# A hybrid RG-LRU / band-attention layer on one core: a fourth plain up pair, other memory and ScalarE order for deferred blocks, a tail without GpSimd

## The chip, the core and the metric

The kernel runs on one NeuronCore of a Trainium2 chip. The metric is the device time of one execution in microseconds; smaller is better. The times below are runs of the kernel before, and one further execution was recorded by the profiler.

## What is computed

One layer of a streaming encoder, for 1024 prompt tokens and 64 sample tokens, all in 32-bit floats:

- u = x·(1 + scale1(c)) + shift1(c), then z = u @ w_in, split into seven sections of 1024 columns.
- Branch A is a gated linear recurrence behind a short convolution, branch B is attention over a band of chunks; x1 = LN(α·x + (1 + gate1)·(merged @ w_out)).
- u2 = x1·(1 + scale2(c)) + shift2(c), then y = LN(α·x1 + (1 + gate2)·(relu(u2 @ w_up + b_up)² @ w_down + b_down)).

The change lies in the last line, the feed-forward part: w_up is 1024 x 4096 and w_down 4096 x 1024. Keys, values and recurrence states are outputs too; the change does not touch them.

## The kernel before

The 1088 tokens are cut into three groups of 384, 384 and 320 (g = 0, 1, 2); features lie on the 128 partitions, in blocks of 128. Every product is made of three matmuls on numbers split into a high and a low part (`mm3`, L109 to L112): high·high, high·low, low·high. A split is a ScalarE copy into the high part and a VectorE subtraction for the low part: for weights L97 and L98 in `wsplit`, for other data L103 and L104 in `split`. `wsplit` also issues the load of the weight block on SP (L93).

**The up product (L610 to L826).** The 32 blocks of w_up's columns are handled as 16 pairs p. Pairs 0 and 1 run beside the end of the first layer norm. Then `up_pair` (L782) takes p = 2 to 15. For groups 0 and 1 a pair is a 2 x 2 product of matrices (two weight blocks by two token groups), which is done in one of two ways:

- a *plain* pair (p < PLAIN, here only p = 2): four products c11, c12, c21, c22 over all 8 feature blocks, each 24 matmuls of 384 columns, each followed by bias, relu and square on ScalarE (`relu2`, L616 and L617);
- a *Strassen* pair: seven products of 12 matmuls (`strassen`, L759), on sums of weights (`wops`, L725: four GpSimd additions L741 to L745, and two more splits) and on sums of tokens, the T tiles of L692 to L720. The products go to banks x, z, x, y, x, y, x, and the product k = 2 adds to bank x after ScalarE has copied x away (L801, L806, L808).

The T tiles are made once, in two halves q, by VectorE additions (L704 to L719) and splits. `vsums` holds one instruction of each half; `tc.issue_after(ins)` means that what the block issues on the engine of `ins` is queued behind `ins` on it (order only, no wait for its end). So plain weights are queued on VectorE behind the first half's x = y - x (L712), Strassen weights behind the second half's.

Group 2 (320 tokens) of each pair goes through `up_g2` (L771): two products ug of 24 matmuls, relu and square into a tile cg, and a store of it into `hg_d` on the ScalarE queue. For groups 0 and 1 `put_pair` (L629) makes the GpSimd sums t1 to t4 and stores seven operands into `hs_d`, four from the GpSimd queue and three from the ScalarE queue.

**The down product (L829 to L911).** It adds up 32 blocks into accumulators: `fg` for group 2, `facc` for groups 0 and 1, loaded from `facc_d` and first scaled and shifted by ScalarE (L863, L900). Group 2's down blocks are the *deferred blocks* of this text: `down_g2` (L848) runs twice, for chunks c = 0, 1 ahead of the Strassen part and for c = 2, 3 behind it. A call goes over r = 0, 1 (four accumulators each), the two chunks and b = 0 to 3; each of its 16 blocks dg is 24 matmuls of 320 columns on one weight block wh_dg, wl_dg and on the operand halves ophg, oplg, which `load_hg` (L843) loads from `hg_d` on SP and splits. Pair 15 (LATE) is special: its `up_g2` is called at L878, after the first two `load_hg`, so TensorE has work while the down product starts.

**Order and memory.** The order on each engine is drawn up at build time by a scheduler, which places each instruction by its readiness in an estimate and by program order; engines run their queue in order. The tiles of the pool `hp` (L829) lie over memory that the up product's pools used: each new tile waits for the last readers of the bytes under it. `hp` gives out memory in the order in which tags are first asked for: facc, opr, oph, opl, then cg, which LATE's `up_g2` takes from `spool[0]`, and so on.

**The tail (L959 to L973).** Behind the last down blocks `final2` normalises group 2's three token tiles (c = 0, 128, 256): for columns 512 and up two VectorE operations (L967, L968) and a store on the ScalarE queue; for the lower half ScalarE's scaling (L966), a multiplication and an addition (L971, L972), by GpSimd for c = 0 and by VectorE else, and a store on SP (L973). The power in the layer norm's moments (L530) is GpSimd's.

Of the kernel before, what the change touches and what calls it, by code (L numbers as in the profile page):

```python
# [11 lines left out]
F32 = mybir.dt.float32  # L12
R32 = mybir.dt.float32r
AF = mybir.ActivationFunctionType
ALU = mybir.AluOpType
PSUM = bass.MemoryType.PSUM

P = 128
# [7 lines left out]
TW2 = 320  # L26
# [22 lines left out]
def body(nc, tc, a):  # L49
    V, S, G, TE, SY = nc.vector, nc.scalar, nc.gpsimd, nc.tensor, nc.sync  # L50
    with ExitStack() as es:
# [34 lines left out]
        for g in range(3):  # L86
            uh[g], ul[g] = newact(g, f"uh{g}"), newact(g, f"ul{g}")

        wlast = [None]

        def wsplit(src, nm, pool=None, tags=("whi", "wlo")):
            raw = wp.tile([P, NB, P], F32, tag="wraw", name=f"wr_{nm}")
            wlast[0] = SY.dma_start(raw, src).ins  # L93
            bufs = 2 if pool else 3
            hi = (pool or wp).tile([P, NB, P], R32, tag=tags[0], bufs=bufs, name=f"wh_{nm}")
            lo = (pool or wp).tile([P, NB, P], R32, tag=tags[1], bufs=bufs, name=f"wl_{nm}")
            S.activation(hi, raw, AF.Copy)  # L97
            V.tensor_tensor(lo, raw, hi.bitcast(F32), op=ALU.subtract)  # L98
            return hi, lo

        def split(hi, lo, src, scl=None):
            if scl is None:
                S.activation(hi, src, AF.Copy)  # L103
                V.tensor_tensor(lo, src, hi.bitcast(F32), op=ALU.subtract)  # L104
            else:
                S.activation(hi, src, AF.Copy, scale=scl)
                V.scalar_tensor_tensor(lo, src, scl, hi.bitcast(F32), op0=ALU.mult, op1=ALU.subtract)
# [591 lines left out]
        for q in range(2):  # L699
            k2 = slice(2 * q, 2 * q + 2)  # L700
            x, y, z = tts.pop() if tts else tt3(q)

            def join(d, b):
                V.tensor_tensor(d, whole(b[0][:, k2, :]), whole(b[1][:, k2, :]), op=ALU.add)  # L704

            def tsplit(k, src):
                split(ut[k][0][:, k2, :], ut[k][1][:, k2, :], src)

            join(x, b11)
            join(y, b12)  # L710
            join(z, b22)
            vsums.append(V.tensor_tensor(x, y, x, op=ALU.subtract).ins)  # L712
            V.tensor_tensor(y, z, y, op=ALU.subtract)
            V.tensor_tensor(z, z, x, op=ALU.subtract)
            tsplit(2, z)
            tsplit(1, x)
            join(x, b21)
            tsplit(3, y)
            V.tensor_tensor(x, x, z, op=ALU.subtract)  # L719
            tsplit(4, x)  # L720
        uops = [b11, b21, ut[2], ut[1], ut[3], b22, ut[4]]

# [48 lines left out]
        def up_g2(p, wa, wb):  # L771
            for b, (wt, f) in enumerate(zip((wa, wb), fblocks(p))):
                ps = acc(f"ug{p}_{b}")
                for kb in range(NB):
                    mm3(ps[:, :TW2], wt[0][:, kb, :], wt[1][:, kb, :], u2h[2][:, kb, :], u2l[2][:, kb, :], kb == 0, kb == NB - 1)
                c = spool[0].tile([P, TW2], F32, tag="cg", bufs=2, name=f"cg{p}_{b}")
                relu2(c, ps[:, :TW2], f)
                put_g2(p, b, c)

        PLAIN, LATE = 3, 15  # L780

        def up_pair(p):  # L782
            f1, f2 = fblocks(p)
            c11, c12, c21, c22 = (new_t(f"c{p}_{k}") for k in range(4))
            if p < PLAIN:
                with tc.issue_after(vsums[0]):
                    wa, wb = up_w(f1), up_w(f2)
                for c, f, g, (wh, wl) in ((c11, f1, 0, wa), (c12, f1, 1, wa), (c21, f2, 0, wb), (c22, f2, 1, wb)):
                    ps = acc(f"up{f}_{g}")
                    for kb in range(NB):  # L790
                        mm3(ps[:, :GW], wh[:, kb, :], wl[:, kb, :], u2h[g][:, kb, :], u2l[g][:, kb, :], kb == 0, kb == NB - 1)
                    relu2(c, ps[:, :GW], f)
                up_g2(p, wa, wb)
                put_pair(p, c11, c12, c21, c22, [], new_t)
                return
            with tc.issue_after(vsums[1]):
                w, wa, wb = wops(a["w_up"][f1], a["w_up"][f2], f"u{p}_", True)

            def after(k, ps):
                if k == 0:  # L800
                    S.activation(c11, ps, AF.Copy)  # L801
                elif k == 1:
                    V.tensor_tensor(c11, ps, c11, op=ALU.add)
                    relu2(c11, c11, f1)
                elif k == 2:
                    S.activation(c12, ps, AF.Copy)  # L806
                elif k == 3:
                    S.activation(c22, ps, AF.Copy)  # L808
                elif k == 4:
                    V.tensor_tensor(c22, ps, c22, op=ALU.add)  # L810
                    relu2(c22, c22, f2)
                elif k == 5:
                    V.tensor_tensor(c12, ps, c12, op=ALU.add)
                    relu2(c12, c12, f1)
                else:
                    relu2(c21, ps, f2)

            strassen(w, uops, f"u{p}", after)
            put_pair(p, c11, c12, c21, c22, [], new_t)
            if p == LATE:  # L820
                return wa, wb
            up_g2(p, wa, wb)
# [10 lines left out]
        def new_facc(fb):  # L833
            return hp.tile([P, TS2], F32, tag=f"facc{fb}", name=f"facc{fb}")

        facc = {fb: new_facc(fb) for fb in range(4)}

        def op_split(src, nm):
            hl = [hp.tile(list(src.shape), R32, tag=t, bufs=7, name=f"{t}{nm}") for t in ("oph", "opl")]
            split(*hl, src)  # L840
            return hl

        def load_hg(c, h):  # L843
# [4 lines left out]
        def down_g2(cs, hg, after):  # L848

            for r in range(2):  # L850
                ps = [acc(f"dg{4 * r + b}_{cs[0]}") for b in range(4)]
                for c in cs:
                    for b in range(4):
                        with tc.issue_after(loads[1]):
                            wh, wl = wsplit(a["w_down"][c, 4 * r + b], f"dg{r}_{c}_{b}")
                        if b == 1 and (c + 1, 0) not in hg and c + 1 in cs:
                            with tc.issue_after(wlast[0]):
                                hg.update({(c + 1, h): load_hg(c + 1, h) for h in range(2)})
                            with tc.issue_after(loads[-1]):
                                SY.dma_start(fg, facc_d[:, :, TS2:T])  # L860
                            for fb in range(NB):
                                for c0, c1, w in parts(2):
                                    S.activation(fg[:, fb, c0:c1], fg[:, fb, c0:c1], AF.Identity, scale=sA[:, fb:fb + 1],  # L863
                                                 bias=bA[:, fb, w:w + 1])
                        for k in range(8):
                            o = hg[c, k // 4]
                            mm3(ps[b][:, :TW2], wh[:, k, :], wl[:, k, :], o[0][:, k % 4, :], o[1][:, k % 4, :],
                                c == cs[0] and k == 0, c == cs[-1] and k == 7)
                            if k == 4:
                                after(r, c, b)  # L870
                        if c == cs[-1]:
                            fb = 4 * r + b
                            for c0, c1, w in parts(2):
                                fc = fg[:, fb, c0:c1]
                                V.scalar_tensor_tensor(fc, ps[b][:, c0:c1], ada[:, G2, fb, w:w + 1], fc, op0=ALU.mult, op1=ALU.add)

        hg = {(0, h): load_hg(0, h) for h in range(2)}
        up_g2(LATE, *wt)  # L878
        fg = actb.tile([P, NB, TW2], F32, tag="act", bufs=2, name="fg")
        down_g2((0, 1), hg, lambda r, c, b: None)  # L880

# [77 lines left out]
        def final2():  # L959
# [5 lines left out]
            for c, cw, y, pt, mean, rstd, nb in done:  # L965
                S.activation(y[:cw, lo], y[:cw, lo], AF.Identity, bias=nb, scale=rstd)  # L966
                V.scalar_tensor_tensor(y[:cw, hi], pt[:cw, :], mean, lg[:cw, hi], op0=ALU.subtract, op1=ALU.mult)  # L967
                V.scalar_tensor_tensor(y[:cw, hi], y[:cw, hi], rstd, lb[:cw, hi], op0=ALU.mult, op1=ALU.add)  # L968
                S.dma_start(a["y"][TS2 + c:TS2 + c + cw, hi], y[:cw, hi])
                e = G if c == 0 else V  # L970
                e.tensor_tensor(y[:cw, lo], y[:cw, lo], lg[:cw, lo], op=ALU.mult)  # L971
                e.tensor_tensor(y[:cw, lo], y[:cw, lo], lb[:cw, lo], op=ALU.add)  # L972
                SY.dma_start(a["y"][TS2 + c:TS2 + c + cw, lo], y[:cw, lo])  # L973

        hg = {(c, h): load_hg(c, h) for c in (2, 3) for h in range(2)}
# [82 lines left out]
```

## Time and profile before

| | us |
|---|---|
| runs shown (three) | 1754.93, 1756.43, 1756.43 |
| median | 1756.43 |
| the profiled execution, its own time | 1756.89 |
| its span, first to last instruction | 1755.1 |
| TensorE busy | 1706.2 (97% of the span) |
| VectorE, ScalarE, GpSimd busy | 1015.1, 782.8, 417.8 |
| mean granted TensorE clock | 0.988 |

Times in the rows are microseconds from the span's start. PE is TensorE's matmuls, PEld its weight loads, DVE VectorE, ACT ScalarE, POOL GpSimd, SP the SyncE queue; ACTq, POOLq and SPq mark queue instructions such as the issue of a transfer. L110 is line 110 of the kernel. Buffer numbers and the pair's number are left out of tile names: `xu` is bank x of an up pair, `wh_dg` the high part of a deferred block's weights. "[4.28 <-ACT c L801]" is the time the engine sat idle just before, and what ended it. The granted clock is a share of full speed, 1.00 being 2.4 GHz and 0.50 being 1.2 GHz. Matmuls are pipelined, so one shown as 0.33 us starts 0.17 us after the one before.

### The profile page before, as it was taken

To read this page: it belongs to the slowest core of one execution; us is meant where nothing else is said; L and a number is where in the kernel's file an instruction comes from. 1 tells how busy PE (TensorE), PEld (TensorE's weight loads), DVE (VectorE), ACT (ScalarE), POOL (GpSimd) and SP (SyncE) were. 2 spreads that over 40 slices of the span, in tenths; PEclk is the share of its full clock that TensorE was granted. 3 is DMA by queue.
4 is the path that set the end of the run, shared out by engine and by line. 5 is a ranking of instruction groups with operands and counts; after the bars stand their busy time and mean duration, and the time that the engine had idled before them with its cause. 6 is when DMAs were issued, how large, how long until landed. Compare 5 with 4: busy or idle time off the path is not lost.

```text
span 1755.1 us, 26600 instructions
## 1 busy us (share of the span) xinstructions
PE 1706.2 (97%) x10620; PEld 1670.8 (95%) x10620; DVE 1015.1 (58%) x1608; ACT 782.8 (45%) x1174; POOL 417.8 (24%) x414
## 2 busy tenths in 40 slices
PE   7999999999999999999999999999999799999995
PEld 4999999999999999999899998999999799999995
DVE  4585553745537465364657758333332567898865
ACT  2452543625335253443534445555554653344342
POOL 1100010000100000000022235565554034443324
PEclk8999999999999999999999999999999899999998
DMA  9242312222121222211156542333334773444442
GB/s 355 94 131 69 101 50 88 67 68 92 56 99 59 69 82 69 98 51 62 64 164 206 185 135 92 127 129 130 129 121 139 283 262 120 175 175 168 156 162 90
DMA packets 88044, 218.08 MB, mean 124 GB/s; under 512 B 11504, under 2 KB 42480, under 8 KB 87920
## 3 DMA queue, kind: packets, MB, share of 16 engines
q1 hardware_dynamic: 71936, 188.46, 31.7%
q10 hardware_dynamic: 11888, 15.34, 2.5%
q0 software_dynamic: 4096, 12.59, 2.0%
q8 instruction: 83, 1.36, 0.3%
q14 instruction: 41, 0.34, 0.1%
HBM read 171.53 MB, written 44.83 MB: 123 GB/s over the span
## 4 chain that ended last, share of the span: by engine, by line
PE 86%; issue 6%; DVE 4%; DMA 2%; ACT 1%; POOL 0%; POOLq 0%; SPq 0%; ACTq 0%; DVEq 0%
PE z L112 13%; PE z L111 13%; PE z L110 13%; PE po L407 3%; PE s L396 2%; PE xu L110 2%; PE xu L111 2%; PE xu L112 2%; PE xd L110 2%; PE xd L112 2%; PE op L110 2%; PE op L112 2%; PE xd L111 2%; PE op L111 2%; PE ug L110 2%
## 5 line engine op out<-in xcount | busy, mean ns | idle before, releaser
L110 PE MATMUL z<-uh,wh_in 128*128 128x384 f32 (+1 forms) x1320 | 436.6, 331 | 3.0 <-ACT uh L103 3.0
L111 PE MATMUL z<-ul,wh_in 128*128 128x384 f32 (+1 forms) x1320 | 437.0, 331 | 0.6 <-DVE ul L104 0.6
L112 PE MATMUL z<-uh,wl_in 128*128 128x384 f32 (+1 forms) x1320 | 436.0, 330 | 0.0
L110 PEld LDWEIGHTS z<-uh,wh_in 128*128 128x128 f32 x1320 | 248.7, 188 | 6.4 <-ACT uh L103 4.0
L111 PEld LDWEIGHTS z<-ul,wh_in 128*128 128x128 f32 x1320 | 248.6, 188 | 4.7 <-DVE ul L104 2.6
L112 PEld LDWEIGHTS z<-uh,wl_in 128*128 128x128 f32 x1320 | 248.6, 188 | 4.0 <-issue 3.1
L97 ACT ACTIVATE wh_in<-wr_in 128x1024 fp32r<-128x1024 f32 x56 | 59.4, 1060 | 96.4 <-PE z L111 91.4
L98 DVE TENSOR_TENSOR wl_in<-wr_in,wh_in 128x1024 fp32r<-128x1024 f32 x56 | 68.4, 1222 | 40.3 <-ACT wh_in L97 40.2
L110 PE MATMUL dg<-ophg,wh_dg 128*128 128x320 f32 x256 | 81.7, 319 | 9.1 <-ACT wh_dg L97 9.1
L112 PE MATMUL dg<-ophg,wl_dg 128*128 128x320 f32 x256 | 80.6, 315 | 1.1 <-DVE wl_dg L98 1.1
L111 PE MATMUL dg<-oplg,wh_dg 128*128 128x320 f32 x256 | 80.3, 314 | 0.0
L160 DVE SCALAR_TENSOR_TENSOR ap<-ar,sil,ap 128x512 f32<-128x512 f32 x112 | 79.9, 745 | 0.0
L456 POOL MEMSET er<- 128x1 f32 x8 | 1.1, 135 | 297.2 <-DVE rt L452 297.2
L104 DVE TENSOR_TENSOR slo_u<-sr_u,shi_u 128x1024 fp32r<-128x1024 f32 x26 | 31.8, 1226 | 68.5 <-ACT shi_u L103 68.5
L379 ACT ACTIVATE pr<-pr,st 128x640 f32<-128x640 f32 (+2 forms) x64 | 44.7, 698 | 57.6 <-DVE st L378 57.4
L362 DVE COPY v<-vt 128x512 f32<-128x512 f32 x16 | 11.1, 692 | 97.0 <-PE vt L361 97.0
L103 ACT ACTIVATE shi_d<-sr_d 128x1024 fp32r<-128x1024 f32 x32 | 33.8, 1057 | 73.6 <-PE yd L111 60.7
L104 DVE TENSOR_TENSOR opl<-op,oph 128x1536 fp32r<-128x1536 f32 x28 | 59.6, 2130 | 12.1 <-ACT oph L103 12.0
L403 ACT ACTIVATE pts<-pt 128x512 f32<-128x512 f32 (+2 forms) x64 | 33.2, 518 | 74.5 <-PE pt L401 73.5
L407 PE MATMUL po<-pts,v 128*128 128x128 f32 x480 | 64.1, 275 | 0.5 <-ACT pts L403 0.3
L110 PE MATMUL ug<-u2h,whi_u 128*128 128x320 f32 x208 | 64.5, 310 | 0.0
L112 PE MATMUL ug<-u2h,wlo_u 128*128 128x320 f32 x208 | 64.5, 310 | 0.0
(384 smaller groups left out, 4574.7 us busy)
## 6 DMA issues: line engine op xcount, KB each, us to landing
wr_in<-in_w_in SPq DMA_DIRECT2D x56, 512.0 KB, 3.3
ar<-in_w_ada SPq DMA_DIRECT2D x46, 512.0 KB, 5.1
op<-hs_d SPq DMA_DIRECT2D x28, 768.0 KB, 5.1
wr_u<-in_w_up SPq DMA_DIRECT2D x33, 512.0 KB, 3.5
wr_dg<-in_w_down SPq DMA_DIRECT2D x32, 512.0 KB, 3.9
wr_d<-in_w_down SPq DMA_DIRECT2D x32, 512.0 KB, 4.0
wr_o<-in_w_out SPq DMA_DIRECT2D x24, 512.0 KB, 3.4
hs_d<-t POOLq DMA_DIRECT2D x64, 192.0 KB, 2.4
```

The costliest lines, as they stand in the source:

```text
L97: S.activation(hi, raw, AF.Copy)
L98: V.tensor_tensor(lo, raw, hi.bitcast(F32), op=ALU.subtract)
L103: S.activation(hi, src, AF.Copy)
L104: V.tensor_tensor(lo, src, hi.bitcast(F32), op=ALU.subtract)
L110: TE.matmul(ps, wh, xh, start=first, stop=False, skip_group_check=more)
L111: TE.matmul(ps, wh, xl, start=False, stop=False, skip_group_check=more)
L112: TE.matmul(ps, wl, xh, start=False, stop=last, skip_group_check=more)
L160: V.scalar_tensor_tensor(part[:, w, :], raw[:, j, :], sil[:, kb, w:w + 1], part[:, w, :], op0=ALU.mult, op1=ALU.add)
L379: S.activation(pr[:rows, :W], pr[:rows, :W], AF.Exp, bias=st[:rows, 0:1], scale=-1.0, accum_out=st[:rows, 1:2])
L396: TE.matmul(sps[:, bk, :cw], qq[:, q0:q0 + P], kk[:, P * j0 + c0:P * j0 + c0 + cw], start=(ip == 0), stop=(ip == 2))
L403: S.activation(pts[:, :min(W, 512)], pt[:, :min(W, 512)], AF.Copy)
L407: TE.matmul(po[:, :P], v[:, j0 + j, :], pts[:, P * j:P * j + P], start=(j == 0), stop=(j == nk - 1))
```

## The change

- PLAIN becomes 4: pair 3 is computed plainly too. `vsums` now holds two instructions per half; pair 2's weights stay behind the first half's x = y - x, pair 3's plain weights go behind the second half's, and the Strassen weights behind the second half's x = x - z (L719), which is the last of VectorE's sums.
- The two cg tiles of the LATE pair are taken from `hp` first of all, ahead of facc; the others stay in `fp`.
- The weights of the first deferred block are loaded and split ahead of LATE's `up_g2` (`pre`), and what that call issues on ScalarE is queued behind the first ophg split and behind that weight split.
- The scaling of `fg` is traced at the second chunk's first block (after its weights) and not at the first chunk's second block; the load of `fg` stays where it was.
- In `final2` VectorE does the multiplication and the addition for all three token tiles.

```diff
-        wlast = [None]
+        wlast, hlast = [None], [None]
...
-            S.activation(hi, raw, AF.Copy)
+            hlast[0] = S.activation(hi, raw, AF.Copy).ins
...
-            V.tensor_tensor(x, x, z, op=ALU.subtract)
+            vsums.append(V.tensor_tensor(x, x, z, op=ALU.subtract).ins)
             tsplit(4, x)
...
-                c = spool[0].tile([P, TW2], F32, tag="cg", bufs=2, name=f"cg{p}_{b}")
+                c = cgs[b] if p == LATE else fp.tile([P, TW2], F32, tag="cg", bufs=2, name=f"cg{p}_{b}")
...
-        PLAIN, LATE = 3, 15
+        PLAIN, LATE = 4, 15
...
-                with tc.issue_after(vsums[0]):
+                with tc.issue_after(vsums[2 * (p - 2)]):
                     wa, wb = up_w(f1), up_w(f2)
...
-            with tc.issue_after(vsums[1]):
+            with tc.issue_after(vsums[3]):
                 w, wa, wb = wops(a["w_up"][f1], a["w_up"][f2], f"u{p}_", True)
...
+        cgs = [hp.tile([P, TW2], F32, tag="cg", bufs=2, name=f"cgl{b}") for b in range(2)]
         facc = {fb: new_facc(fb) for fb in range(4)}
+        hi_ins = []
...
-            split(*hl, src)
+            hi_ins.append(split(*hl, src))
...
-                            wh, wl = wsplit(a["w_down"][c, 4 * r + b], f"dg{r}_{c}_{b}")
+                            wh, wl = pre.pop() if pre else wsplit(a["w_down"][c, 4 * r + b], f"dg{r}_{c}_{b}")
                         if b == 1 and (c + 1, 0) not in hg and c + 1 in cs:
...
                                 SY.dma_start(fg, facc_d[:, :, TS2:T])
+                        if b == 0 and c == 1 and r == 0:
                             for fb in range(NB):
...
-        up_g2(LATE, *wt)
+        with tc.issue_after(loads[1]):
+            pre = [wsplit(a["w_down"][0, 0], "dg0_0_0")]
+        with tc.issue_after(hi_ins[0]), tc.issue_after(hlast[0]):
+            up_g2(LATE, *wt)
...
-                e = G if c == 0 else V
-                e.tensor_tensor(y[:cw, lo], y[:cw, lo], lg[:cw, lo], op=ALU.mult)
-                e.tensor_tensor(y[:cw, lo], y[:cw, lo], lb[:cw, lo], op=ALU.add)
+                V.tensor_tensor(y[:cw, lo], y[:cw, lo], lg[:cw, lo], op=ALU.mult)
+                V.tensor_tensor(y[:cw, lo], y[:cw, lo], lb[:cw, lo], op=ALU.add)
```

## Rows read from the trace of the kernel before

**Rows 1.** The page's busy times: us, share of the span, instructions.
```profile
PE 1706.2 (97%) x10620; PEld 1670.8 (95%) x10620; DVE 1015.1 (58%) x1608; ACT 782.8 (45%) x1174; POOL 417.8 (24%) x414
```

**Rows 2.** TensorE's waits over the span: us in total, times, longest.
```profile
PE dg L110 <- ACT wh_dg L97: 9.1, 3, 5.3
...
PE dg L112 <- DVE wl_dg L98: 1.1, 1, 1.1
```

**Rows 3.** Windows behind three waits: length, busy by engine, granted clock, DMA share, GB/s.
```profile
1086.80:1092.60 5.80, 5.71 (x19) 5.71 (x20) 3.96 (x3) 1.35 (x4) 3.98 (x5) 0.52 0.73 217
...
1370.50:1376.00 5.50, 4.23 (x15) 3.83 (x16) 4.68 (x5) 3.33 (x4) 0.00 (x0) 0.53 0.84 263
...
1388.00:1394.00 6.00, 5.61 (x26) 5.33 (x27) 5.12 (x4) 6.00 (x6) 0.00 (x0) 0.72 0.68 210
```

**Rows 4.** Timeline of TensorE, up product: start, us, engine, line, operation, idle before.
```profile
1063.00 0.33 PE L112 MATMUL up<-u2h,wl_u 128*128 128x384 f32 x1
...
1065.08 0.33 PE L112 MATMUL up<-u2h,wl_u 128*128 128x384 f32 x1
...
1076.56 0.34 PE L112 MATMUL xu<-u2h,wlo_u 128*128 128x384 f32 x1
...
1086.89 0.69 PE L110 MATMUL xu<-T2h,shi_u 128*128 128x384 f32 x1 [4.28 <-ACT c L801]
```

**Rows 5.** Timeline of ScalarE and VectorE ahead of pair 3's first summed operand.
```profile
1082.82 0.84 ACT L103 ACTIVATE T4h<-tt 128x768 fp32r<-128x768 f32 x1 [3.41 <-DVE tt L719]
...
1086.36 0.47 ACT L801 ACTIVATE c<-xu 128x384 f32<-128x384 f32 x1
...
1086.59 1.75 DVE L104 TENSOR_TENSOR T4l<-tt,T4h 128x768 fp32r<-128x768 f32 x1
```

**Rows 6.** Timeline of ScalarE and VectorE where the deferred blocks begin.
```profile
1363.53 0.53 ACT L616 ACTIVATE cg<-ug,bup 128x320 f32<-128x320 f32 x1 [3.97 <-DMA hs_d<-t]
...
1367.29 2.43 ACT L103 ACTIVATE ophg<-hg 128x1280 fp32r<-128x1280 f32 x2 [0.53 <-ACT cg L617]
1369.62 2.93 ACT L97 ACTIVATE wh_dg<-wr_dg 128x1024 fp32r<-128x1024 f32 x3
...
1380.28 6.70 ACT L863 ACTIVATE fg<-fg,bA,sA 128x256 f32<-128x256 f32 x16 [2.16 <-DMA fg<-facc_d]
...
1368.59 2.89 DVE L104 TENSOR_TENSOR oplg<-hg,ophg 128x1280 fp32r<-128x1280 f32 x2 [11.70 <-ACT ophg L103]
1371.40 1.22 DVE L98 TENSOR_TENSOR wl_dg<-wr_dg,wh_dg 128x1024 fp32r<-128x1024 f32 x1
```

**Rows 7.** Timelines of GpSimd and SP there; page's transfers (KB, us to landing).
```profile
1362.75 1.63 POOL L638 DMA_DIRECT2D hs_d<-t  x3
...
hs_d<-t POOLq DMA_DIRECT2D x64, 192.0 KB, 2.4
...
1371.89 0.58 SPq L860 DMA_DIRECT2D fg<-facc_d  x1
```

**Rows 8.** Windows over the deferred blocks: columns as in rows 3.
```profile
1344.00:1412.00 68.00, 57.21 (x347) 55.69 (x346) 28.09 (x29) 38.85 (x56) 9.34 (x14) 0.92 0.79 282
1380.00:1388.00 8.00, 4.58 (x33) 4.32 (x31) 0.05 (x1) 7.72 (x18) 0.00 (x0) 1.00 1.03 420
1396.00:1408.00 12.00, 12.00 (x84) 12.00 (x83) 8.61 (x12) 4.67 (x4) 0.00 (x0) 1.00 0.96 337
```

**Rows 9.** The tail: line L531 (ns min/median/max), then timelines of GpSimd, VectorE, SP.
```profile
L531 DVE SCALAR_TENSOR_TENSOR lmvb<-lmvb x3: 143/147/1215, 1742.1 to 1743.6; 128x1 f32<-128x1 f32 x2, 64x1 f32<-64x1 f32 x1
...
1744.88 4.13 POOL L972 TENSOR_TENSOR y<-y,lgb 128x512 f32<-128x512 f32 x1
...
1745.40 1.28 DVE L971 TENSOR_TENSOR y<-y,lgb 128x512 f32<-128x512 f32 x2
...
1749.03 1.42 SPq L973 DMA_DIRECT2D out_y<-y  x3
```

**Rows 10.** A window over pairs 4 to 14: columns as in rows 3.
```profile
1092.60:1347.00 254.40, 254.40 (x1554) 254.40 (x1553) 81.34 (x82) 134.66 (x225) 147.77 (x140) 1.00 0.36 123
```

More of the change, by code (lines that the diff above doesn't have):

```diff
@@ L102, in split @@
             if scl is None:
-                S.activation(hi, src, AF.Copy)
+                first = S.activation(hi, src, AF.Copy).ins
                 V.tensor_tensor(lo, src, hi.bitcast(F32), op=ALU.subtract)
+                return first
             else:
```

## The prediction

> **What bounds the kernel now.** I read the busy shares first: TensorE 97% of the span, every other engine under 60% [rows 1]. So only three things count: what is added to TensorE's work, where it stands still, and where it runs at the lower of its two clock levels. Then TensorE's own waits: the first matmuls of the deferred blocks waited 9.1 us for ScalarE's weight split, 5.3 of them at once, and 1.1 us for VectorE's [rows 2]; and pair 3, the first Strassen pair, stood 4.28 us behind a ScalarE copy [rows 4]. Last the windows behind these waits [rows 3]: granted clock 0.52, 0.53 and 0.72 where it is 1.00 elsewhere, so each longer wait is paid a second time at 1.2 instead of 2.4 GHz. The sum is made against the profiled execution, 1756.9 us (span 1755.1), 0.5 above the median of the runs.
>
> **The fourth plain pair.** A plain pair has 4 products of 24 matmuls, a Strassen pair 7 of 12: 96 against 84. Twelve of this width start from 1063.00 to 1065.08, 2.08 us [rows 4], so TensorE gets +2.08 us. What goes: pair 3's first matmul on a summed operand starts at 1086.89 after 4.28 us idle [rows 4], and the next 5.8 us ran at clock 0.52 [rows 3], a loss of 5.8 x 0.48 = 2.8. The chain behind it: ScalarE's in-order queue stood 3.41 us before the split T4h, waiting for VectorE's L719; the copy that TensorE needed, c at L801, stood behind that split, ended at 1086.83, and TensorE followed [rows 5]. In the changed kernel pair 3 needs no summed operand. Its matmuls start where xu started, 1076.56 [rows 4], and take 96 x 0.173 plus 48 deferred ones at 0.145 (84 in 12 us, two of them cut by the edges [rows 8]), 23.6 us: pair 4 asks for the sums at about 1100, while VectorE's last write of them ended at 1088.3 [rows 5]. That is 12 us of cover. The two weight sums and splits of pair 3 (POOL, ScalarE, VectorE) vanish too; pair 3's plain weights and pair 4's move behind later sums in VectorE's queue and lie under the same 12 us. Nothing is late next that I can see. **Term: 2.1 - 4.3 - 2.8 = -5.0 us**; bounds -5.0 and, if the wait moves along, +2.1.
>
> **Memory and ScalarE order of the deferred blocks.** Now ScalarE first finishes pair 15's deferred blocks: bias and square, two store issues, then the splits ophg from 1367.29 and wh_dg from 1369.62 [rows 6]; TensorE's first dg matmul waits 5.3 of the 9.1 us for these. The first relu there started late, 3.97 us idle until a store hs_d<-t landed [rows 6]: its tile cg lies where the c and t tiles of pair 15 were. The data was there before: the ophg splits were held by ScalarE's own queue (idle 0.53 <- cg L617 [rows 6]), not by a load, and the first wr_dg load stands right behind the hg loads on SP, in the changed kernel too. With both issue_after blocks the splits come first. ScalarE is free at 1359.6 (where that idle stretch began); two ophg splits (2.43) and one wh_dg (1.0 of 2.93 for three) end near 1363.1, VectorE's counterparts (1.45 twice, 1.2 once [rows 6]) by 1365.0; the last ug matmul ends at about 1365.4 (first dg, 1370.7, less 5.3). So dg can follow without a gap. What is queued behind the new order: cg's four activations and two ACT-queue stores, about 2.5 us, which only feed a store, and behind them wh_dg of the second block, near 1368 instead of 1366.
>
> The accumulators' scaling is 16 activations, 6.70 us from 1380.28 [rows 6], after a load that SP issued at 1371.89, 8.4 us before [rows 7]. The fourth block's weight split stands behind it, and TensorE waited the other 3.8 us of [rows 2]. Traced at the second chunk, the scaling loses its precedence to the weights of blocks 3 and 4; what it can still hold up is the block after.
>
> What these waits cost: 5.3 + 1.1 + 3.8 us idle. The slow stretches: 15 matmuls took 4.23 us where 0.145 each make 2.2 [rows 3], a loss of 2.0; 26 took 5.61, a loss of 1.8. Together 14.0 us. I don't take all of it. The second block's weights end at about 1369.3 against a need at 1369.1 (0.2). The fourth block is needed at 1375.6; its load queues on SP behind hg1 and fg and lands near 1374 if fg's 8.4 us repeats from 1365.3, so its lo half is ready near 1376.3: 0.8. Scaling plus three weight splits are 9.7 us of ScalarE in about 10: 1.5. That leaves 2.5 us, between 0 and 5.6 (3.8 + 1.8, nothing gained at the second wait). **Term: -14.0 + 2.5 = -11.5 us**, bounds -14.0 and -8.4.
>
> **The transfers behind it.** From 1344 to 1412 the DMA engines moved 282 GB/s over 68 us, 19.2 MB [rows 8]. With 14 us taken out that must pass in 54 us, 355 GB/s. The trace shows 420 over 8 us and 337 over 12 us with a share of 0.96, the smaller packets of op among them [rows 8]. At 337 it takes 57 us, 3 us too long; I take no loss, as 420 was held when the same hg, fg and weight loads were in flight.
>
> **VectorE alone in the tail.** POOL's two operations of the first token tile end at 1749.0, the second one 4.13 us long; SP's three stores wait for that, then issue one after another [rows 9]. VectorE's tiny L531 took 1.22 us while POOL ran L971, against 0.15 for the other two [rows 9], so VectorE is 1.1 us late as well. With all six operations on VectorE: it reaches L971 at about 1744.3 (1745.40 less 1.1), six at 0.64 end at 1748.1. The last store is issued there instead of at about 1750.0. **Term: -1.9 us**, bounds -0.8 (the 1.1 stays) and -2.4.
>
> The Trainium skill, page "Perfetto Trace Analysis", section "Optimizing Scalar/DVE Operations", says that work may be offloaded from a saturated VectorE to GpSimd, which speaks against this move, though it adds that the shared read port can spoil it. By the first half the tail would be 1.3 us longer on VectorE and the sum 1739.8; the 4.13 us row follows the second half.
>
> **Sum.** -5.0 - 11.5 - 1.9 = -18.4: 1756.9 - 18.4 = **1738.5 us**; its own range, with the bounds, 1735 to 1743.
>
> **The rivals.**
> *The new memory blocks VectorE.* With cg in front, facc, opr, oph and opl all lie 2 x 1280 B higher, so the last opl buffer reaches into the c tiles, where cg waited for the store [rows 6]. If hg's second half uses it, its subtraction waits until pair 15's last store lands, about 1366.8 (three issued over 1.63 us from 1362.75, plus the median 2.4 to landing [rows 7]), and the first wl_dg stands behind it: dg's third matmul at about 1369.4 instead of 1365.6, 3.8 idle and about 2 of slow clock. 1744. For: cg did wait there. Against: the buffer is one of seven. 0.15.
> *The transfers bind.* 3 us more, 1741.5. For: share 0.96 at 337 GB/s; against: 420. 0.1.
> *The first Strassen pair's wait moves along.* It was a queue order, not a late sum: pair 4's first copy may stand behind splits again. +7.1: 1745.6. Against: the split it stood behind waited for sums that now have 12 us. 0.1.
> *Slower: the x bank loses its cover.* In each Strassen pair the next product into bank x waits for ScalarE's copy out of it; deferred ug matmuls put in between hide that. Without them pair 3 lost 4.28 [rows 4]. The whole order is made anew, so all 12 remaining pairs could lose cover, at 0 to 4.28 us each: in the middle, 2.14, 25.7 us, 1764.2. It decides from (18.4 + 3.5) / 12 = 1.8 us a pair. Against: from 1092.6 to 1347 TensorE was busy 254.40 of 254.40 us [rows 10], and pair 3's deferred blocks remain as cover. 0.06.
> That the change doesn't do what it says: the new edges bind ScalarE's order only and may change nothing at the second wait; that is the upper bound -8.4 above.
>
> **How the numbers follow.** Forecast 0.57, rivals 0.15, 0.1, 0.1, 0.06, and 0.02 for a stall elsewhere in the new order, too small to matter. The range 1734 to 1747 holds the forecast, the bounds and the first three rivals. A measurement tells about 0.2% (3.5 us) from no change: faster 0.92, same 0.02, slower 0.06.
>
> **What would show it.** Right: no wait of xu near 1087 and clock 1.00 there; ophg and the first wh_dg ahead of cg's relu on ScalarE; dg following ug within 1 us; fg's scaling behind the fourth block's weights; no POOL work after L530 in the tail. Wrong: dg's L112 waiting for VectorE with oplg before it held by a store; a wait at the first T operand of pair 4; xu waiting for L806 in many pairs.

## The result and the profile after

The changed kernel took 1744.17 us in the median (four runs, 1741.14 to 1744.71) where the kernel before took 1755.68 beside it: ratio 0.9931, 95% interval 0.9914 to 0.9948. The forecast was 1738.5; the range, 1734 to 1747, holds the result. The profiled execution took 1744.55 us, its span 1742.8, so 12.3 less than before and not 18.4. Lines of the code lie 1 to 7 further down: L112 of before is L113, the store's L973 is L979.

The busy times of the page, against [rows 1]: TensorE has 2.5 us less to do, although twelve matmuls came in, because less of it runs at the low clock.

```profile
PE 1703.7 (98%) x10632; PEld 1668.7 (96%) x10632; DVE 1008.6 (58%) x1605; ACT 779.9 (45%) x1169; POOL 403.3 (23%) x408
```

TensorE's timeline from pair 15 into the deferred blocks, the waits alone. The wait of 4.28 us near 1087 [rows 4] is gone; the first line here is pair 15's x bank, which waited 0.63 at 1351.84 before, 5.1 us later. Of the deferred blocks' waits [rows 2] the 5.3 us one is gone, but dg's third matmul, which had waited 1.1, waits 4.78:

```profile
1346.74 0.44 PE L111 MATMUL xu<-T3h,shi_u 128*128 128x384 f32 x1 [0.63 <-ACT c L807]
...
1365.39 0.58 PE L113 MATMUL dg<-ophg,wl_dg 128*128 128x320 f32 x1 [4.78 <-DVE wl_dg L98]
...
1380.21 0.42 PE L111 MATMUL dg<-ophg,wh_dg 128*128 128x320 f32 x1 [2.75 <-ACT wh_dg L97]
...
1381.15 0.42 PE L111 MATMUL dg<-ophg,wh_dg 128*128 128x320 f32 x1 [0.38 <-ACT wh_dg L97]
```

Windows, columns as in [rows 3]. The first covers the up stage where pair 3 used to wait: full and at clock 1.00. The second lies behind the new wait: 24 matmuls took 5.11 us, 1.6 more than 24 at 0.145. In the third the transfers fill the engines. The fourth lies behind the second wait, which was followed by 0.72 before and by 1.00 now:

```profile
1075.00:1101.00 26.00, 26.00 (x160) 26.00 (x160) 12.43 (x9) 13.59 (x23) 19.92 (x18) 1.00 0.41 139
1365.00:1370.50 5.50, 5.11 (x24) 5.11 (x25) 4.62 (x5) 1.27 (x1) 0.00 (x0) 0.69 0.98 317
1370.50:1376.00 5.50, 5.50 (x40) 5.50 (x39) 0.88 (x1) 3.49 (x9) 0.00 (x0) 1.00 1.05 422
1380.00:1386.00 6.00, 5.41 (x35) 5.13 (x36) 5.17 (x4) 6.00 (x7) 0.00 (x0) 1.00 0.62 181
```

Timelines of ScalarE, VectorE, GpSimd and SP at the deferred blocks, answering to [rows 6, 7]. ScalarE's splits now come first (1354.86, 1357.20) and nothing holds them. VectorE's two oplg, which ran in a row before, are 5 us apart: the second starts at 1362.71, and the first wl_dg, which TensorE waits for, stands behind it. GpSimd issues pair 15's last stores from 1358.49. The release shown for the second oplg (cgl L618) has nothing to do with it; the store is the last thing it needs, see the second run below. Further down the scaling of fg still stands ahead of the fourth block's split (1379.12), as before:

```profile
1354.86 2.44 ACT L103 ACTIVATE ophg<-hg 128x1280 fp32r<-128x1280 f32 x2 [0.40 <-ACT c L618]
1357.20 1.04 ACT L97 ACTIVATE wh_dg<-wr_dg 128x1024 fp32r<-128x1024 f32 x1
...
1368.59 1.27 ACT L103 ACTIVATE ophg<-hg 128x1280 fp32r<-128x1280 f32 x1 [3.94 <-DMA hg<-hg_d]
1372.51 6.70 ACT L867 ACTIVATE fg<-fg,bA,sA 128x256 f32<-128x256 f32 x16 [2.65 <-DMA fg<-facc_d]
1379.12 2.94 ACT L97 ACTIVATE wh_dg<-wr_dg 128x1024 fp32r<-128x1024 f32 x3
...
1356.17 1.49 DVE L104 TENSOR_TENSOR oplg<-hg,ophg 128x1280 fp32r<-128x1280 f32 x1 [4.38 <-ACT ophg L103]
1362.71 1.49 DVE L104 TENSOR_TENSOR oplg<-hg,ophg 128x1280 fp32r<-128x1280 f32 x1 [5.05 <-ACT cgl L618]
1364.12 3.49 DVE L98 TENSOR_TENSOR wl_dg<-wr_dg,wh_dg 128x1024 fp32r<-128x1024 f32 x3
...
1358.49 1.63 POOL L639 DMA_DIRECT2D hs_d<-t  x3
...
1364.65 0.58 SPq L863 DMA_DIRECT2D fg<-facc_d  x1
```

The tail, against [rows 9]: VectorE does all six operations, and SP's three stores are issued as they come; the last issue ends at 1740.05, 2.7 us ahead of the span's end.

```profile
1737.73 2.32 SPq L979 DMA_DIRECT2D out_y<-y  x3
1738.23 1.28 DVE L978 TENSOR_TENSOR y<-y,lgb 128x512 f32<-128x512 f32 x2
```

### The profile page after: what moved, and what is told of

Its sections match the earlier page's. It is cut to its first block, busy times and chain, and to the rows that moved or that the text cites. A ratio compares the mean times of both kernels' runs of the same rounds, so it can differ in the third digit from the quotient of the medians.

```text
span 1742.8 us, 26601 instructions
## 1 busy us (share of the span) xinstructions
PE 1703.7 (98%) x10632; PEld 1668.7 (96%) x10632; DVE 1008.6 (58%) x1605; ACT 779.9 (45%) x1169; POOL 403.3 (23%) x408
## 4 chain that ended last, share of the span: by engine, by line
PE 91%; DVE 3%; DMA 2%; issue 2%; ACT 2%; POOL 0%; SPq 0%; DVEq 0%; ACTq 0%; POOLq 0%
PE z L113 13%; PE z L112 13%; PE z L111 13%; PE po L408 3%; PE s L397 2%; PE dg L111 2%; PE dg L113 2%; PE xd L111 2%; PE dg L112 2%; PE xd L113 2%; PE xd L112 2%; PE xu L111 2%; PE xu L112 2%; PE xu L113 2%; PE op L113 2%
## 5 line engine op out<-in xcount | busy, mean ns | idle before, releaser
L112 PE MATMUL z<-ul,wh_in 128*128 128x384 f32 (+1 forms) x1320 | 437.0, 331 | 0.8 <-DVE ul L104 0.8
L113 PE MATMUL z<-uh,wl_in 128*128 128x384 f32 (+1 forms) x1320 | 436.0, 330 | 0.0
L112 PEld LDWEIGHTS z<-ul,wh_in 128*128 128x128 f32 x1320 | 248.6, 188 | 4.9 <-DVE ul L104 2.8
L113 PEld LDWEIGHTS z<-uh,wl_in 128*128 128x128 f32 x1320 | 248.6, 188 | 4.0 <-issue 3.1
L113 PE MATMUL dg<-ophg,wl_dg 128*128 128x320 f32 x256 | 79.8, 313 | 4.8 <-DVE wl_dg L98 4.8
L112 PE MATMUL dg<-oplg,wh_dg 128*128 128x320 f32 x256 | 79.7, 311 | 0.0
L104 DVE TENSOR_TENSOR wlo_u<-wr_u,whi_u 128x1024 fp32r<-128x1024 f32 x24 | 34.7, 1447 | 56.7 <-ACT whi_u L103 56.7
L408 PEld LDWEIGHTS po<-pts,v 128*128 128x128 f32 x480 | 61.2, 191 | 1.2 <-ACT pts L404 1.2
```

Of the source, the lines that this page charges most:

```text
L112: TE.matmul(ps, wh, xl, start=False, stop=False, skip_group_check=more)
L113: TE.matmul(ps, wl, xh, start=False, stop=last, skip_group_check=more)
L408: TE.matmul(po[:, :P], v[:, j0 + j, :], pts[:, P * j:P * j + P], start=(j == 0), stop=(j == nk - 1))
```

## The experiments

Runs of one kernel differ by 1 to 5 us: the profiled executions reach the start of pair 2 between 1035.2 and 1038.0, ahead of any line that was edited. So besides the medians I compare four stages of each profiled execution: *up* (from TensorE's first matmul after its wait near 1037 to pair 15's x bank, the 0.63 us wait), *deferred* (to the first xd matmul), *main* (to the last yt) and *tail* (to the span's end). Three executions have the same code up to the tail or nearly so (after, run 4, run 8): their deferred stage took 80.0, 79.1 and 78.8, their main stage 302.3, 303.5 and 301.9. Differences under some 1.2 us in the first, and 1.6 in the second, say nothing.

| run | median us, before beside it | ratio, interval | up | deferred | main | tail |
|---|---|---|---|---|---|---|
| before | | | 314.2 | 84.2 | 301.5 | 17.5 |
| after | 1744.2, 1755.7 | 0.9931, 0.9914 to 0.9948 | 309.2 | 80.0 | 302.3 | 13.8 |
| 1 memory | 1746.0, 1756.8 | 0.9938, 0.9924 to 0.9952 | 309.2 | 81.7 | 302.3 | 13.7 |
| 2 queue | 1742.1, 1756.8 | 0.9918, 0.9904 to 0.9931 | 309.2 | 78.6 | 302.2 | 13.7 |
| 3 cg late | 1740.9, 1756.8 | 0.9913, 0.9900 to 0.9927 | 310.7 | 79.2 | 302.3 | 13.7 |
| 4 tail undone | 1747.4, 1756.8 | 0.9950, 0.9937 to 0.9962 | 309.2 | 79.1 | 303.5 | 17.6 |
| 5 plain alone | 1752.8, 1756.4 | 0.9976, 0.9967 to 0.9985 | 309.2 | 84.1 | 302.1 | 17.5 |
| 6 scaling late | 1743.7, 1756.4 | 0.9927, 0.9914 to 0.9941 | 310.7 | 79.4 | 302.8 | 13.7 |
| 7 memory, scaling | 1743.6, 1756.4 | 0.9926, 0.9913 to 0.9938 | 309.2 | 80.0 | 302.5 | 13.8 |
| 8 scaling old | 1743.1, 1756.4 | 0.9926, 0.9914 to 0.9939 | 309.2 | 78.8 | 301.9 | 13.7 |
| 9 fg late | 1740.3, 1757.1 | 0.9904, 0.9889 to 0.9918 | 309.2 | 77.3 | 302.4 | 13.7 |
| 10 and memory | 1740.8, 1757.1 | 0.9906, 0.9891 to 0.9921 | 309.2 | 77.2 | 301.8 | 13.7 |
| 11 and queue | 1738.0, 1757.1 | 0.9890, 0.9873 to 0.9906 | 309.2 | 74.3 | 302.8 | 13.7 |
| 12 and op held | 1740.2, 1757.5 | 0.9903, 0.9886 to 0.9919 | 309.2 | 72.3 | 305.8 | 13.8 |

**Run 1: the memory of oplg.**

```diff
-        facc = {fb: new_facc(fb) for fb in range(4)}
+        facc = {fb: new_facc(fb) for fb in range(3)}
```

> The changed kernel with one allocation moved: the accumulator facc3 is taken later, so everything behind it in the deferred blocks' pool lies 3072 B lower and the last opl buffer no longer reaches into the c tiles of pair 15. Nothing else is edited. Theory 'memory' (the second half's subtraction waits for the tile t15_1 that a store still reads, and the first wl_dg stands behind it on VectorE): the second oplg starts right behind the first, near 1357.7 instead of 1362.71; dg's third matmul loses its 4.78 us wait and the 5.5 us behind it run at clock 1.00 instead of 0.69 (1.6 us): 6.4 us less to that point. The second wait (2.75 + 0.38) may grow, since TensorE comes 6.4 us sooner and fg's load only about 5 us sooner: between 0 and 2 given back. 1738 to 1740 us. Rival 'transfers' (the data of hg's second half or of the first weights is what is late): no change, 1744.2, with the same 4.78 us wait, then with a DMA named as what ended VectorE's idle time.

Half of it came true: the wait went, but the time, 1746.0, is 6 us above the range. The first lines are TensorE's timeline, the others ScalarE's and SP's; the window below has the columns of [rows 3]:

```profile
1361.44 0.42 PE L113 MATMUL dg<-ophg,wl_dg 128*128 128x320 f32 x1 [1.06 <-DVE wl_dg L98]
...
1379.30 0.63 PE L111 MATMUL dg<-ophg,wh_dg 128*128 128x320 f32 x1 [7.33 <-ACT wh_dg L97]
...
1371.61 6.69 ACT L867 ACTIVATE fg<-fg,bA,sA 128x256 f32<-128x256 f32 x16 [3.73 <-DMA fg<-facc_d]
...
1350.99 0.81 SPq L848 DMA_DIRECT2D hg<-hg_d  x2
...
1361.01 0.58 SPq L863 DMA_DIRECT2D fg<-facc_d  x1
```

```profile
1372.00:1378.00 6.00, 0.00 (x0) 0.00 (x0) 0.00 (x0) 6.00 (x16) 0.00 (x0) 0.78 1.03 423
```

With the buffer elsewhere the first wait shrinks from 4.78 to 1.06: the memory was its cause. (The edit moves more than oplg: the buffers that hg is loaded into lie elsewhere too, and its first loads are issued at 1350.99 instead of 1341.95. Run 3, in which they keep their time, takes the wait away as well.) But the whole of it comes back at the second one, 7.33 us. TensorE now asks there 5.5 us sooner (1371.97 for 1377.46), and the load of fg, issued 3.6 us sooner than in the changed kernel, lets the scaling start only 0.9 us sooner (1371.61 for 1372.51): the transfer engines are full (share 1.03), and the fourth block's split stands behind the scaling. I had allowed 0 to 2 us of this.

**Run 2: the order on VectorE.** The subtraction of hg's second half is put behind the first weights'; the rest of the edit only lets that be said.

```diff
+            if mid:
+                mid()
...
+                hi_ins.append(S.activation(hl[0], o, AF.Copy).ins)
+                with tc.issue_after(llast[0]):
+                    V.tensor_tensor(hl[1], o, hl[0].bitcast(F32), op=ALU.subtract)
+                return hl
             return op_split(o, f"g{c}_{h}")
```

> The changed kernel with its memory as it is, and one order turned on VectorE: the subtraction of hg's second half is issued behind the first weights' (wl_dg). Theory 'memory': the second half's subtraction still starts only near 1362.7, but wl_dg now ends near 1358.9, so dg's third matmul does not wait; instead the matmuls on the second half (the 13th on, at about 1362.1) wait until that subtraction ends near 1364.0, about 1.9 us, and the slow stretch behind is shorter: 1740.5 us, between 1739 and 1742. Rival 'transfers': wl_dg is as late as before, 1744.2. If the in-order queue were not the link, the third matmul would still wait 4.78 us.

VectorE's timeline, then TensorE's:

```profile
1361.55 1.49 DVE L854 TENSOR_TENSOR oplg<-hg,ophg 128x1280 fp32r<-128x1280 f32 x1 [3.28 <-DMA hs_d<-t]
...
1363.10 0.43 PE L112 MATMUL dg<-oplg,wh_dg 128*128 128x320 f32 x1 [1.94 <-DVE oplg L854]
```

As the memory theory has it: the wait moves to the second half's matmuls and is 1.94 us, where about 1.9 was expected; the time, 1742.1, lies at the upper end of the range. And with wl_dg out of the way the trace names what the subtraction waits for, the store of a t tile. The second wait (2.66 us) stayed. The order of SP's loads was made anew as well, though no line of the edit asks for it: the second chunk's two hg loads, which follow each other in the changed kernel (1357.69), now have weights between them (1356.34, 1358.30, 1363.07). The first block's loads come before that, so its wait is not touched by this.

**Run 3: cg where it was.** The line `cgs = ...` moves behind the first two `load_hg`.

> The changed kernel with the two cg tiles of pair 15 taken where the kernel before has them, behind the opl buffers, on top of the c and t tiles; the ScalarE order edit stays. Theory 'memory': oplg's second half is free as in the kernel before, so dg's third matmul does not wait (-6.4); ScalarE's bias-relu into cg waits for pair 15's last store, until about 1362.5 to 1364, and the second block's weights stand behind it: about 1 us of wait at dg's 25th matmul. About 1739 us, between 1737.5 and 1741: then the move of cg cost more than it brought. Rival 'cg's wait costs as much as in the kernel before': the block behind waits 3 to 5 us, 1743 or more.

The two short waits came as expected (0.48 and 0.70 us), but the second wait was 4.96 us, and the deferred stage, 79.2, is not told from the changed kernel's. (The profiled execution, 1743.1 us, is the slowest of the four; the others took 1740.8 to 1741.0, the upper end of the range expected, but the intervals overlap.) ScalarE's timeline shows cg paying what it paid in [rows 6], now behind the splits and so at no cost to the first block:

```profile
1356.58 1.04 ACT L97 ACTIVATE wh_dg<-wr_dg 128x1024 fp32r<-128x1024 f32 x1
1362.02 0.95 ACT L617 ACTIVATE cgl<-ug,bup 128x320 f32<-128x320 f32 x2 [4.40 <-DMA hs_d<-t]
```

So the order edit alone does what order and memory do together; the move of cg brought nothing that these runs can show.

**Run 4: the tail undone** (`e = G if c == 0 else V` back in `final2`).

> The changed kernel with the first token tile's two last operations back on GpSimd, nothing else. By the prediction's term (the last store is issued 1.9 us sooner): 1744.2 + 1.9 = 1746.1. By the two traces as a whole (the last store issued 11.9 us behind the last dg matmul instead of 13.8, and the span's end 2.7 us behind that issue instead of 4.6): 1744.2 + 3.8 = 1748.0. Rival 'VectorE alone was no gain': 1744.2.

1747.4, 3.2 us above the changed kernel in the medians and 3.8 in the tail stage (17.6 for 13.8). The stage, which does not hold the scatter of what comes before, speaks for the larger of the two figures. GpSimd and SP in its timeline:

```profile
1735.35 4.13 POOL L979 TENSOR_TENSOR y<-y,lgb 128x512 f32<-128x512 f32 x1
...
1739.50 1.42 SPq L980 DMA_DIRECT2D out_y<-y  x3
```

The last issue ends at 1740.92 and the span at 1745.6, 4.7 later, against 2.7 without GpSimd.

**Run 5: the fourth plain pair alone**, on the kernel before (`PLAIN = 4` and the `vsums` edits).

> The kernel before with the fourth plain pair alone (and the weight loads issued behind the later sums, as in the change); memory, ScalarE order and tail stay as before. Theory 'term of its own': the 4.28 us wait near 1087 and the slow stretch behind it go, twelve matmuls come: -5.0, about 1750.7 us; the waits of the deferred blocks (9.1 and 1.1 us) stay, each 5 us sooner. Rival 'the wait moves along': 1756 or more.

The up stage takes 309.2 for 314.2, to the hundredth as in the changed kernel (309.17), and the other stages are those of before, their waits too:

```profile
1364.68 0.63 PE L110 MATMUL dg<-ophg,wh_dg 128*128 128x320 f32 x1 [5.25 <-ACT wh_dg L97]
...
1381.88 0.41 PE L110 MATMUL dg<-ophg,wh_dg 128*128 128x320 f32 x1 [3.17 <-ACT wh_dg L97]
```

The medians show 3.5 us, and the interval (1.5 to 3.3 thousandths, 2.6 to 5.8 us) holds the 5.0.

**Run 6: the scaling behind the second chunk's first weights** (`with tc.issue_after(hlast[0]):` around it).

> The changed kernel with the scaling of the accumulators issued on ScalarE behind the first weights of the second chunk (and so behind the fourth block's), memory as it is. Theory 'scaling still stands ahead of the fourth block's weights': the wait of 2.75 + 0.38 us near 1380 goes, the one of 4.78 us stays: 1741.1 us, between 1740.5 and 1742.5. Rival 'the fourth block waits for its load anyway': 1744.2.

No gain, as the rival has it. The wait near 1380 went, but 1.67 us and two of 0.4 came at 1385 to 1391, behind the scaling in its new place; and the fourth block's split now stood idle for its own load, 3.55 us. The 3.1 us that I expected back was the wait of one execution; see run 8 for its scatter.

**Run 7: both.**

> Both edits together: facc3 taken later, and the scaling behind the second chunk's first weights. Theory 'two separate waits': both go, -6.4 and -3.1, 1734.7 us, between 1734 and 1737. Rival 'the transfers bind': with both gone the loads from 1344 to 1412 must pass in 9.5 us less, and a wait on a DMA appears at the second chunk's first block or at the op tiles: 1738 or more.

The rival is right in that a load is late, though it is the fourth block's and not the second chunk's first. It was issued at 1360.85, just behind fg's 1.31 MB, and the split that needs it started at 1372.23:

```profile
1372.23 1.06 ACT L97 ACTIVATE wh_dg<-wr_dg 128x1024 fp32r<-128x1024 f32 x1 [5.24 <-DMA wr_dg<-in_w_down]
```

**Run 8: the scaling traced where it was** (the line `if b == 0 and c == 1 and r == 0:` taken out).

> The changed kernel with the scaling traced where the kernel before has it, nothing else. Theory 'moving it changed nothing': ScalarE's order stays the same, with the scaling ahead of the fourth block's weights: 1744.2 us within 0.1%. By the prediction (the scaling loses its precedence when traced at the second chunk): about 2 to 4 us slower, 1746 to 1748.

The same, and in its trace the scaling stands where it stands in the changed kernel. That part of the change did nothing.

This run also shows how far one execution of the same order can be trusted. TensorE's timeline, then a window behind the first wait:

```profile
1364.36 0.63 PE L113 MATMUL dg<-ophg,wl_dg 128*128 128x320 f32 x1 [4.60 <-DVE wl_dg L98]
...
1378.19 0.41 PE L111 MATMUL dg<-ophg,wh_dg 128*128 128x320 f32 x1 [0.54 <-ACT wh_dg L97]
...
1379.13 0.41 PE L111 MATMUL dg<-ophg,wh_dg 128*128 128x320 f32 x1 [0.39 <-ACT wh_dg L97]
```

```profile
1364.36:1370.36 6.00, 6.00 (x22) 6.00 (x23) 5.11 (x4) 1.27 (x1) 0.00 (x0) 0.50 0.96 356
```

The first wait is that of the changed kernel (4.78), but the 6 us behind it ran at clock 0.50, where the profile after has 0.72, and the second wait is 0.93 us, where it has 3.13. Run 4 is the same: 4.66 us, 0.52, then 1.37 us. Counted from pair 15's x bank, TensorE comes 1.0 us later to the second wait, having lost more behind the first, and the fourth block's split starts 1.2 us sooner.

**Run 9: fg's load behind the second chunk's first weights**, its scaling in four parts.

```diff
-                            with tc.issue_after(loads[-1]):
-                                SY.dma_start(fg, facc_d[:, :, TS2:T])
-                        if b == 0 and c == 1 and r == 0:
-                            for fb in range(NB):
...
+                        if c == 1 and r == 0:
+                            if b == 0:
+                                with tc.issue_after(wlast[0]):
+                                    SY.dma_start(fg, facc_d[:, :, TS2:T])
+                            with tc.issue_after(hlast[0]):
+                                for fb in (2 * b, 2 * b + 1):
...
```

> The changed kernel, memory as it is, with the load of fg (1.31 MB) issued on SP behind the first weights of the second chunk instead of ahead of the fourth block's, and its scaling cut in four parts of 4 activations, each behind the weight split of one block of the second chunk. Theory 'the second wait belongs to the transfers and to the scaling together' (the run with the scaling late had the fourth block's split waiting for its own load, behind fg's on the same queue; the run with the memory moved had 7.33 us of wait there): the fourth block's weights come about 3 us sooner (1.31 MB at 420 GB/s) and nothing stands ahead of their split, so the wait of 2.75 + 0.38 us goes; the first wait of 4.8 us and its slow stretch stay: 1741 us, between 1740 and 1742. Rival 'the loads cannot come faster, whatever their order': 1744.

As expected: no wait is left near 1380, the 4.68 us of the first remain, deferred 77.3.

**Runs 10 and 11: the same with run 1's memory, then with run 2's order too.**

> The same with facc3 taken later, so that oplg's second half is free. Theory 'two causes, each hides the other': now the gain of the memory shows, which it did not alone (1746.0): against that run the 7.33 us wait and about 3 us of slow clock behind it go, 1735.7 us, between 1735 and 1738; only the 1.06 us at dg's third matmul stay. Rival 'the loads cannot come faster': the wait at the fourth block or the one behind stays at 4 to 7 us, 1741 or more.

> The same as the run before, with the first weights' subtraction on VectorE ahead of that of hg's second half. Theory: the last 1.06 us at dg's third matmul go, 1734.7 us, between 1734 and 1737. Rival: the second half's subtraction comes 1.2 us later and TensorE waits for it at the 14th matmul instead: no change against the run before.

Run 10 missed by 5 us. ScalarE and TensorE in its timeline:

```profile
1368.57 1.06 ACT L97 ACTIVATE wh_dg<-wr_dg 128x1024 fp32r<-128x1024 f32 x1 [1.79 <-DMA wr_dg<-in_w_down]
...
1380.66 1.47 ACT L103 ACTIVATE oph<-op 128x1536 fp32r<-128x1536 f32 x1
1382.03 1.04 ACT L97 ACTIVATE wh_dg<-wr_dg 128x1024 fp32r<-128x1024 f32 x1
...
1383.12 0.42 PE L111 MATMUL dg<-ophg,wh_dg 128*128 128x320 f32 x1 [1.64 <-ACT wh_dg L97]
...
1385.11 0.63 PE L113 MATMUL dg<-ophg,wl_dg 128*128 128x320 f32 x1 [1.42 <-DVE wl_dg L98]
```

The fourth block's split starts 3.7 us sooner than in run 7 and no longer holds anyone. But three blocks on, ScalarE makes the main blocks' splits and scalings first (4.6 us from 1377.44, the last of them shown), and a third wait of 3.06 us, with 18 matmuls in 4.89 us at clock 0.50 behind it, takes back what the first wait had given up (4.68 to 1.06 us and its slow stretch). Run 11 has 0.22, 1.06 and 0.70 us left of these waits. It is 3.3 us above its expectation and still the fastest, 1738.0 us; its interval, 0.9873 to 0.9906, lies wholly below the changed kernel's. What gave the 2.9 us that its deferred stage has over run 10's stays open: as in run 2, the loads of the second chunk's hg came apart on SP too (1358.62 and 1361.71, in run 10 both from 1357.83).

**Run 12: the main blocks' first loads held too.**

```diff
-                with tc.issue_after(wloads[-1] if c == 0 and k > 4 else loads[-1]):
+                with tc.issue_after(held[0] if c == k == 0 else wloads[-1] if c == 0 and k > 4 else loads[-1]):
```

> The run before (fg late, memory moved, first weights ahead) with the loads of the main blocks' first operands (op, facc) issued on SP behind the first weights of the second half of the deferred blocks, about 8 us later. Theory 'what stood ahead of the last weights were the main blocks' splits and loads': the waits of 1.06 and 0.70 us near 1383 and about 1.7 us of slow clock behind them go: 1734.6 us, between 1734 and 1736. Rival 'the op splits only come late elsewhere': the same time in waits of the main blocks' first matmuls near 1415 to 1427, 1738 or more.

The rival again: deferred falls to 72.3, the 72.7 that my forecast amounted to or a little better, and main rises by 3.1 over run 11's. TensorE's waits from 1405 to 1435:

```profile
PE xd L113 <- DVE wlo_d L104: 2.0, 1, 2.0
PE dg L113 <- DVE wl_dg L98: 1.1, 1, 1.1
PE yd L113 <- DVE slo_d L104: 0.6, 1, 0.6
```

## Why the prediction was right or wrong

The direction and the range were right; the likeliest case was not. Span against span, -12.3 is -0.1 at the start, -5.0 up, -4.2 deferred, +0.8 main and -3.8 tail, where I had -5.0, -11.5, 0 and -1.9.

- **The fourth plain pair: right**, -5.0 as summed, shown alone by run 5. No Strassen pair lost its cover (TensorE busy 247.40 of 247.40 us from 1092.6 to 1340), and no wait moved along.
- **ScalarE's order: right.** The splits ran first and ug ended when dg's first matmul could start (1360.15). Run 3 shows that this edit needs no memory moved.
- **"VectorE's counterparts by 1365.0, so dg can follow without a gap": the step that failed.** The second oplg was held, as in the rival "The new memory blocks VectorE", to which I gave 0.15; the store that held it reads a t tile (run 2), where the rival named the c tiles. Its price was 3.8 idle and about 2 of slow clock; it measured 4.78 and 1.6. Its argument against, one buffer of seven, was no argument: the buffer is no matter of chance once the kernel is built. All five profiled executions with this memory and this order on VectorE (after, runs 4, 6, 8 and 9) have the wait, 4.60 to 4.83 us.
- **"The scaling loses its precedence": wrong**, run 8. The second wait fell from 3.81 us to 3.13, and to 1.37 and 0.93 in runs 4 and 8, but with the scaling still ahead of the fourth block's split; what went in all three is the slow clock behind it (1.8).
- **"I take no loss" on the transfers: wrong in what it left out.** The rival priced 3 us of bytes over the whole stretch. What counts is the queue ahead of one load: in run 1 fg's, in runs 6 and 7 the fourth block's came late behind other bytes, with the engines at 400 to 423 GB/s. The Trainium skill, "DMA: Bandwidth & Descriptors", section "Queues, rings and completion order", says that each transfer engine consumes a queue's descriptors in ring order. The trace agrees: with fg's load put behind, the fourth block's split started at 1368.57 (run 10) and not 1372.23 (run 7), although its load was issued only 0.5 us sooner (1360.36 and 1360.85).
- **The tail: right mechanism, mis-sized.** From the last dg matmul to the last store's issue it took 11.89 us for 13.78, the -1.9 of the sum; a second 1.9 us lies behind that issue, where I had changed nothing. The page "Perfetto Trace Analysis" of the Trainium skill, section "Optimizing Scalar/DVE Operations", whose advice to offload work to GpSimd I had weighed against this part, gives it for a saturated VectorE and adds that the shared read port can spoil it. The trace goes with that caution: GpSimd's share cost 3.8 us (run 4). How much of this is the port no run tells.

So the errors were +6.4 (first wait), +0.6 (second wait), +0.8 (main) and -1.9 (tail): 1738.5 + 5.9 = 1744.4, against 1744.55. That the total met the rival's 1744 is in part luck: the other three nearly cancel. And only the first and the last are more than scatter. In runs 4 and 8, the same code up to the tail or nearly so, the first wait with its slow stretch is 7.3 and 7.4 us instead of 6.4, the second wait 1.1 and 1.6 below the 2.5 that I had left for it instead of 0.6 above, and main 1.2 above and 0.4 below the changed kernel's.

Why the first wait is worth so little when it is removed (run 1) is the lesson of the case: behind it stand the transfers (runs 1 and 7), behind these ScalarE's splits (run 10), behind these the main blocks' operands (run 12), each within 5 us of the next. Of the edits to the deferred blocks only those of runs 9 to 12, which all put fg's load and scaling later (10 to 12 with more besides), brought the stage clear of the 78.8 to 80.0 of the changed kernel, and of the times only run 11's has its interval clear of the changed kernel's. Whether a better order of all four exists was not tried.

## What to carry to other kernels

When a tile is allocated earlier, everything behind it in the pool moves: add up the addresses and look for a late reader (a store) of the bytes under the first buffers used. A wait taken off an engine that is nearly always busy is worth at most the distance to the next late thing; list the next two or three (bytes ahead on the queue, work ahead on the splitting engine) before counting it. Put loads on a shared queue in the order in which they are needed, not in which they become possible.

## What the runs showed of the hardware that was not expected

- With GpSimd at work last, the span ends 6.1 us behind its last operation, in both kernels (1749.01 to 1755.1 before, 1739.48 to 1745.6 in run 4, run 5 the same), although the last store's bytes move within 1.5 us of its issue; without it the span ends 2.7 us behind the last store's issue. What passes in that time no row shows.
- A wait of the same length is not always followed by the lower clock. The wait near 1036 is 1.68 us in the profile after and 1.72 in run 3: the window behind it had clock 1.00 in the one and 0.72 in the other, 1.5 us longer in the up stage (310.7 for 309.2; run 6 the same; runs 1, 2 and 4 waited 1.72 too and took 309.2). The second wait was followed by 1.00 after 2.75 us in the changed kernel, by 0.72 after 2.66 in run 2. From there on, the waits of 4.28 to 7.33 us were all followed by less than 1.00 (0.50 to 0.75 over the 6 us behind them); of the shorter ones some were and some were not. So to count a wait twice, as I did, is no safe sum for the short ones, and even for equal long ones the second price differed (1.6 us in the profile after, 2.8 in run 8).
- When VectorE's oplg meets GpSimd's last sum of pair 15, one of the two is slowed, and not always the same one. In run 1 two oplg took 4.22 us and the sum 1.04; in the changed kernel the oplg took its 1.49 and the sum 1.85. What decides it no run shows.
